# Convolution taps that read a projection's products in PSUM, with weight splits of 1024 columns, in the token mixer of a two-block transformer kernel

## The chip, the cores and the metric

The kernel runs on one core of one Trainium2 chip. The metric is the device time of one execution in microseconds, and the number given for a kernel is the median of its runs. The engines are named as the profile names them: PE is TensorE (PEld its weight loads), DVE is VectorE, ACT is ScalarE, POOL is GpSimd and SP is SyncE, which only starts transfers here.

## What is computed

256 tokens of 1024 features go through two blocks. The first is a layer norm, a token mixer, a norm, a mixture of 32 experts (two per token) and a norm; the second has two layers of attention with feed-forward parts. The mixer has two branches, a spatial gating unit and a gated delta rule over eight heads. The part that the change touches makes the delta rule's q, k and v:

```python
proj = h @ w_in + b_in
...
qkv = jax.nn.silu(_causal_dwconv(dn_qkv, dn_conv_w)).astype(jnp.float32)
q, k, vv = jnp.split(qkv, [DN_KEY, 2 * DN_KEY], axis=-1)
...
q = q * lax.rsqrt(jnp.sum(q * q, -1, keepdims=True) + L2_EPS)
k = k * lax.rsqrt(jnp.sum(k * k, -1, keepdims=True) + L2_EPS)
```

The convolution is causal, four taps deep, one filter per feature: token t of a feature is the sum of tokens t-3 to t, each with its own weight, and tokens before the first are zero. The bias `b_in` is added before the convolution, so the zeros ahead of the first token have no bias in them. For all tokens but the first three the bias adds the same constant, bias times the sum of the four weights; for the first three it adds less.

## The kernel before

**Three stretches.** By the timeline the mixer and the norm in front of it take the first 380 us or so, the mixture of experts runs to about 828 us, and the second block takes the rest. The change lies in the mixer.

**A dense** (`dense`, lines 277 to 325) multiplies the tokens by 512 columns of a weight matrix, over eight chunks of 128 features. Its float32 weights arrive in raw tiles of 1 MB (2048 columns, a ring of five buffers) that SP asks for. Each raw tile is split, 512 columns at a time, into a high part `wh` (line 248, a rounding copy by ACT) and a low part `wl`, the rest (line 249, a subtraction by DVE, or by POOL where `lo_eng` says so). The pool `sp` has five buffers of each. A product is then three matmuls: high by high (line 309, or 319), low tokens by high weights (311, or 321), high tokens by low weights (312, or 320). In the form with features on the partitions ("fm") a dense has 96 matmuls of 256 columns, in the form with tokens on them ("tm") 48 of 512. The result stands in one of two PSUM buffers (`pd`, 128 x 1024) until the function `consume` has read it. Smaller products use four PSUM buffers `pt`, which the profile calls ps.

**The convolution stage** (lines 444 to 484) runs six denses, s = 0 to 5: two each for q, k and v. The function `conv` consumes each: ACT copies each quarter of the PSUM buffer with bias into `pre` in SBUF (line 468) and also makes the fourth tap of it, scaled and with bias, in `cv` (line 469); DVE adds the other three taps of each quarter, reading `pre` (line 471, twelve instructions a dense); ACT applies silu (line 473); POOL squares the result for the norms of q and k (line 476). POOL also clears the three zeros ahead of each `pre` (line 463) and makes one low part in four, one in two in dense 0. PE sums the squares (`sums`, lines 453 to 456), four matmuls behind the next dense. `cv` stands in slot 8 and `sq` in slot 9, one buffer each.

**Behind it** come two denses for z and four for the gates, which a list `Z` holds until they are put between the steps of the delta rule: the score matrices (lines 555 to 569), and the inverse of a triangular matrix, first 32 x 32 blocks on DVE, then two levels of products (lines 607 to 635). A step of a level is a product (line 615), a mask by DVE (618), one or two products with the masked one (624, 629), and subtractions by DVE (631, 633). Lines 645 and after use the inverse.

**Order.** Each engine runs its instructions in the order of its own program. A scheduler sets that order when the kernel is built, from priorities and from buffers; the source doesn't write it out. A change of one instruction's engine or size can thus move others on all engines. The mixture of experts fetches its weights into the mixer's slots and the ring as these come free, which is before the mixer's end.

## Time and profile before

| | |
|---|---|
| median of three runs | 1444.41 us (1443.34 to 1444.89) |
| span of the profiled execution | 1444.6 us |
| mixer | 0 to about 380 us |
| mixture of experts | about 380 to 828 us |
| second block | 828 us to the end |

The profile gives for each instruction its start, its duration and, where its engine was idle before it, how long and what ended the wait. The duration of a pipelined instruction overlaps the next one's start, so the time that a run of them takes is the distance of their starts. [...] The windows sum busy time per engine in a stretch. A wait names the last semaphore that came.

### The profile page before, as it was taken

How to read it: one execution, taken by the hardware profiler on the slowest of the kernel's cores; microseconds unless marked ns; L12 is line 12 of the kernel's file. 1: busy time of each engine (PE TensorE's matmuls, PEld its weight loads, DVE VectorE, ACT ScalarE, POOL GpSimd, SP SyncE). 2: the span in 40 equal slices, each digit the busy share in tenths (PEclk: the TensorE clock that was granted, in tenths of full speed). 3: DMA queues.
4: the chain of work that ended last, by engine and by line, in shares of the span. 5: the costliest groups of instructions: out<-in, count | busy, mean ns of one | idle time of the engine just before them, and what ended most of it. 6: DMA issues, size and time to landing. Idle time of an engine off the chain costs nothing.

```text
span 1444.6 us, 24989 instructions
## 1 busy us (share of the span) xinstructions
PE 1254.9 (87%) x10074; PEld 1001.7 (69%) x10077; DVE 760.0 (53%) x1516; ACT 574.6 (40%) x1165; POOL 137.6 (10%) x118
## 2 busy tenths in 40 slices
PE   5999999699588778767778669999999999999997
PEld 4987988698444434324334248779998887899985
DVE  6897955976611111201101078756666568666664
ACT  3775635444201101101101035655555548655553
POOL 2431000400200000000000021410000013100000
PEclk9999999899799979989889879999999999999998
DMA  7453542388599999999999935245554552455550
GB/s 289 146 175 106 205 158 88 121 338 316 210 419 419 419 411 419 419 420 419 419 419 419 420 132 201 88 146 179 184 192 164 197 209 88 146 176 185 194 176 29
DMA packets 58967, 356.18 MB, mean 247 GB/s; under 512 B 13312, under 2 KB 13824, under 8 KB 17632
## 3 DMA queue, kind: packets, MB, share of 16 engines
q1 hardware_dynamic: 57072, 347.09, 63.3%
q0 software_dynamic: 1488, 6.92, 1.3%
q8 instruction: 81, 1.33, 0.4%
q10 hardware_dynamic: 288, 0.52, 0.1%
q14 instruction: 38, 0.31, 0.1%
HBM read 352.68 MB, written 1.84 MB: 245 GB/s over the span
## 4 chain that ended last, share of the span: by engine, by line
PE 34%; DMA 20%; DVE 4%; ACT 2%; issue 1%; POOL 1%; DVEq 0%; SPq 0%; ACTq 0%
DMA xw<-in_w_dram 16%; PE pd L311 7%; PE pd L312 7%; PE pd L309 7%; DMA raw<-in_w_dram 4%; PE pd L320 4%; PE pd L321 4%; PE pd L319 4%; ACT s L1198 1%; PE ps L1221 1%; PE ps L1181 1%; DVE wl L249 1%; PE ps L1215 0%; DVE s L1186 0%; POOL s L1205 0%
## 5 line engine op out<-in xcount | busy, mean ns | idle before, releaser
L248 ACT ACTIVATE wh<-raw 128x512 fp32r<-128x512 f32 (+1 forms) x532 | 331.0, 631 | 332.6 <-PE pd L311 160.0
L249 DVE TENSOR_TENSOR wl<-raw,wh 128x512 fp32r<-128x512 f32 x497 | 357.8, 727 | 190.2 <-ACT wh L248 187.9
L312 PE MATMUL pd<-xh,wl 128*128 128x256 f32 x1232 | 350.2, 284 | 8.6 <-DVE wl L249 7.0
L309 PE MATMUL pd<-xh,wh 128*128 128x256 f32 x1232 | 348.3, 283 | 0.0
L311 PE MATMUL pd<-xl,wh 128*128 128x256 f32 x1232 | 348.2, 283 | 0.0
L312 PEld LDWEIGHTS pd<-xh,wl 128*128 128x128 f32 x1232 | 232.3, 189 | 12.5 <-DVE wl L249 8.5
L309 PEld LDWEIGHTS pd<-xh,wh 128*128 128x128 f32 x1232 | 233.7, 190 | 1.9 <-issue 1.6
L311 PEld LDWEIGHTS pd<-xl,wh 128*128 128x128 f32 x1232 | 233.1, 189 | 1.9 <-issue 1.4
L1004 DVE COPY hs<-ps 128x256 f32<-128x256 f32 x32 | 13.6, 424 | 265.5 <-PE ps L1000 265.5
L1000 PE MATMUL ps<-xw,xe 128*32 128x256 f32 x1568 | 111.8, 392 | 23.8 <-DMA xw<-in_w_dram 22.0
L1000 PEld LDWEIGHTS ps<-xw,xe 128*32 128x32 f32 x1568 | 53.0, 111 | 65.1 <-DMA xw<-in_w_dram 31.7
L1010 ACT ACTIVATE hx<-ps 128x128 f32<-128x128 f32 x32 | 8.9, 277 | 217.0 <-PE ps L1007 217.0
L249 POOL TENSOR_TENSOR wl<-raw,wh 128x512 fp32r<-128x512 f32 (+1 forms) x35 | 52.8, 1511 | 391.8 <-ACT wh L248 374.8
L1021 PE MATMUL pd<-ys,cst 128*32 128x256 f32 x256 | 71.2, 428 | 15.8 <-ACT ys L1019 15.2
L1015 PE MATMUL ps<-xw,hx 128*32 128x256 f32 x752 | 58.6, 457 | 20.7 <-DVE hx L1011 14.5
L1021 PEld LDWEIGHTS pd<-ys,cst 128*32 128x32 f32 x256 | 28.3, 121 | 59.6 <-ACT ys L1019 34.5
L320 PE MATMUL pd<-wl,hh 128*128 128x512 f32 x176 | 68.6, 390 | 0.0
L321 PE MATMUL pd<-wh,hl 128*128 128x512 f32 x176 | 68.6, 390 | 0.0
L319 PE MATMUL pd<-wh,hh 128*128 128x512 f32 x176 | 68.5, 389 | 0.0
L321 PE MATMUL pd<-wh,xl 128*128 128x512 f32 (+2 forms) x144 | 55.4, 385 | 2.6 <-DVE xl L275 2.6
L320 PE MATMUL pd<-wl,xh 128*128 128x512 f32 (+2 forms) x144 | 56.3, 391 | 1.5 <-DVE wl L249 1.5
L1015 PEld LDWEIGHTS ps<-xw,hx 128*32 128x32 f32 x752 | 24.5, 126 | 47.4 <-DVE hx L1011 20.1
(445 smaller groups left out, 1852.0 us busy)
## 6 DMA issues: line engine op xcount, KB each, us to landing
xw<-in_w_dram SPq DMA_DIRECT2D x145, 1024.0 KB, 19.9
raw<-in_w_dram SPq DMA_DIRECT2D x47, 1024.0 KB, 19.9
raw<-in_gu_dram SPq DMA_DIRECT2D x44, 1024.0 KB, 5.0
raw<-in_w_in_dram SPq DMA_DIRECT2D x32, 1024.0 KB, 4.9
raw<-in_dn_dram SPq DMA_DIRECT2D x20, 1024.0 KB, 4.8
raw<-in_e_b_dram SPq DMA_DIRECT2D x6, 1024.0 KB, 5.4
bc<-in_big_dram POOLq DMA_DIRECT2D x8, 512.0 KB, 5.9
raw<-in_w_pb_dram SPq DMA_DIRECT2D x4, 1024.0 KB, 5.0
```

The source lines that it names most:

```text
L248: self.nc.scalar.activation(hi, src, AF.Copy)
L249: (eng or self.nc.vector).tensor_tensor(lo, src, hi.bitcast(F32), op=OP.subtract)
L309: nc.tensor.matmul(o, a, xh[:, kc, :], start=(kc == 0 and oc % 2 == 0), stop=False, skip_group_check=True)
L311: nc.tensor.matmul(o, a, xl[:, kc, :], start=False, stop=False, skip_group_check=True)
L312: nc.tensor.matmul(o, b, xh[:, kc, :], start=False, stop=(kc == nk - 1), skip_group_check=True)
L319: nc.tensor.matmul(o, xh[:, kc, ts], a, start=(kc == 0), stop=False, skip_group_check=True)
L320: nc.tensor.matmul(o, xh[:, kc, ts], b, start=False, stop=False, skip_group_check=True)
L321: nc.tensor.matmul(o, xl[:, kc, ts], a, start=False, stop=(kc == nk - 1), skip_group_check=True)
L1000: T.matmul(ph[32 * c:32 * c + 32, :256], xe[:, kc, ei * 32:ei * 32 + 32], wt[kc // 2][:, kc % 2, c * 256:(c + 1) * 256], start=(kc == 0), ...
L1015: T.matmul(py[32 * c:32 * c + 32, :256], hx[:, fc % 2, (fc // 2) * 32:(fc // 2) * 32 + 32], wt[4 + fc // 2][:, fc % 2, c * 256:(c + 1) * 2 ...
L1021: T.matmul(pz[32 * ei:32 * ei + 32, c * 256:(c + 1) * 256], ident[:, 32 * c:32 * c + 32], ys, start=True, stop=True, skip_group_check=True)
L1181: T.matmul(ps[:, t * 128:t * 128 + 128 * (t + 1)], q[:, t * 128:t * 128 + 128], k[:, :128 * (t + 1)], start=(t == 0 and j == 0), stop=(j = ...
```

## The change

- The copy `pre` and the pool `conv` are gone. DVE's twelve taps read the products in PSUM, without bias, at 253 to 255 columns each (line 480 of the new kernel); the tokens that a shift would leave out are simply not written.
- The bias comes in with the fourth tap: the constant `bw` is now the bias times the sum of all four weights, and a small table `cut` holds what the first three tokens got too much. One subtraction by DVE per dense corrects them (line 475), before the taps.
- The square moves from POOL to ACT (line 485), and all low parts of the stage are made by DVE. POOL has nothing left in the stage.
- In the mixer the splits are 1024 columns wide, with three buffers instead of five; in the second block they stay 512 wide with five.

Behind the convolution the lines of the new kernel are those of before plus 8. The core of the diff:

```diff
-        step = max(1, 512 // ncol)
+        step = max(1, self.wide // ncol)
...
-                wh = self.sp.tile([128, 512], F32R, name="wh", tag="wh")
-                wl = self.sp.tile([128, 512], F32R, name="wl", tag="wl")
+                wh = self.sp.tile([128, self.wide], F32R, name="wh", tag="wh")
+                wl = self.sp.tile([128, self.wide], F32R, name="wl", tag="wl")
...
-            self.sp = pool("sp", 5)
+            self.sp, self.wide = pool("sp", 5), 512
...
-        self.sp = sp_es.enter_context(tc.tile_pool(name="sp", bufs=5))
+        self.sp, self.wide = sp_es.enter_context(tc.tile_pool(name="sp", bufs=3)), 1024
...
-        with tc.tile_pool(name="conv", bufs=2) as cv:
+        if True:
             wc = self.par("conv").rearrange("p (c k) -> p c k", k=4)
             bw = small.tile([128, 24], F32, name="bw")
+            cut = small.tile([128, 24, 3], F32, name="cut")
+            V.tensor_mul(cut[:, :, 2], self.par("b_qkv"), wc[:, :, 0])
+            V.tensor_mul(cut[:, :, 1], self.par("b_qkv"), wc[:, :, 1])
+            V.tensor_add(cut[:, :, 1], cut[:, :, 1], cut[:, :, 2])
+            V.tensor_mul(cut[:, :, 0], self.par("b_qkv"), wc[:, :, 2])
+            V.tensor_add(cut[:, :, 0], cut[:, :, 0], cut[:, :, 1])
             V.tensor_mul(bw, self.par("b_qkv"), wc[:, :, 3])
+            V.tensor_add(bw, bw, cut[:, :, 0])
...
                 def conv(ps, s=s, dst=dst):
-                    pre = cv.tile([128, 4, 260], F32, name="pre", tag="pre")
-                    P.memset(pre[:, :, 0:3], 0.0)
                     c_ = slot("cv", 8, 8, 256)[:, :4]
                     for oc in range(4):
                         c = s * 4 + oc
-                        p_ = ps[:, oc * 256:(oc + 1) * 256]
-                        S.activation(pre[:, oc, 3:259], p_, AF.Identity, bias=self.par("b_qkv", c))
-                        S.activation(c_[:, oc], p_, AF.Identity, bias=bw[:, c:c + 1], scale=wc[:, c, 3:4])
+                        S.activation(c_[:, oc], ps[:, oc * 256:(oc + 1) * 256], AF.Identity, bias=bw[:, c:c + 1],
+                                     scale=wc[:, c, 3:4])
+
+                    V.tensor_tensor(c_[:, :, 0:3], c_[:, :, 0:3], cut[:, s * 4:s * 4 + 4], op=OP.subtract)
+                    for oc in range(4):
+                        c = s * 4 + oc
                         for kk in range(3):
-                            V.scalar_tensor_tensor(c_[:, oc], pre[:, oc, kk:kk + 256], wc[:, c, kk:kk + 1],
-                                                   c_[:, oc], op0=OP.mult, op1=OP.add)
+                            sh = 3 - kk
+                            V.scalar_tensor_tensor(c_[:, oc, sh:], ps[:, oc * 256:(oc + 1) * 256 - sh], wc[:, c, kk:kk + 1],
+                                                   c_[:, oc, sh:], op0=OP.mult, op1=OP.add)
                     S.activation(dst, c_, AF.Silu)
                     if s < 4:
                         sq = slot("sq", 9, 8, 256)[:, :4]
-                        P.tensor_tensor(sq, dst, dst, op=OP.mult)
+                        S.activation(sq, dst, AF.Square)
                         sqs.append((s, sq))
-                self.dense(A["w_in"][4 + s], 512, 8, xh, xl, "fm", conv,
-                           lo_eng=lambda i, s=s: P if i % 4 == 3 or (s == 0 and i % 2) else None)
+                self.dense(A["w_in"][4 + s], 512, 8, xh, xl, "fm", conv)
```

The scheduler's order changes with it. In the rows below, a name with its number is one buffer, and the name left of the arrow is written. On ACT, from the silu of conv 0 on, before:

```order
L473 ACTIVATE q_183<-cv_386 128x1024
L248 ACTIVATE wh_592<-raw_574 128x512
L248 ACTIVATE wh_608<-raw_574 128x512
L248 ACTIVATE wh_624<-raw_574 128x512
L248 ACTIVATE wh_642<-raw_640 128x512
L468 ACTIVATE pre_543<-pd_410,prm_86 128x256
L469 ACTIVATE cv_545<-pd_410,bw_248,prm_86 128x256
```

The silu of a conv and the first reads of the next dense's PSUM buffer have four high parts between them. On ACT, from the last high part ahead of the silu of conv 1 on, after:

```order
L248 ACTIVATE wh_738<-raw_736 128x1024
L482 ACTIVATE q_183<-cv_510 128x1024
L485 ACTIVATE sq_529<-q_183 128x1024
L472 ACTIVATE cv_652<-pd_535,bw_245,prm_86 128x256 x4
L248 ACTIVATE wh_766<-raw_736 128x1024
L248 ACTIVATE wh_822<-raw_820 128x1024
```

Silu and square of a conv now stand directly ahead of the four reads of the next dense's PSUM buffer. On DVE, around the end of conv 3's taps (buffer cv_871), before:

```order
L249 TENSOR_TENSOR wl_969<-raw_966,wh_968 128x512
L471 SCALAR_TENSOR_TENSOR cv_871<-pre_869,prm_86,cv_871 128x256 x11
L249 TENSOR_TENSOR wl_985<-raw_966,wh_984 128x512
L471 SCALAR_TENSOR_TENSOR cv_871<-pre_869,prm_86,cv_871 128x256
L249 TENSOR_TENSOR wl_1001<-raw_966,wh_1000 128x512
L249 TENSOR_TENSOR wl_1064<-raw_1061,wh_1063 128x512
```

A conv's taps come nearly in a block, and low parts follow them. On DVE, from the last taps of conv 1 (buffer cv_510) to those of conv 2 (cv_652), after:

```order
L249 TENSOR_TENSOR wl_739<-raw_736,wh_738 128x1024
L480 SCALAR_TENSOR_TENSOR cv_510<-pd_393,prm_86,cv_510 128x254
L480 SCALAR_TENSOR_TENSOR cv_510<-pd_393,prm_86,cv_510 128x255
L475 TENSOR_TENSOR cv_652<-cv_652,cut_246 128x4x3
L480 SCALAR_TENSOR_TENSOR cv_652<-pd_535,prm_86,cv_652 128x253
L480 SCALAR_TENSOR_TENSOR cv_652<-pd_535,prm_86,cv_652 128x254
L480 SCALAR_TENSOR_TENSOR cv_652<-pd_535,prm_86,cv_652 128x255
```

The last tap of a conv is now followed at once by the next conv's correction, with no low part between them. On PE, in the first of the two levels of the triangular inverse, before (pd_1823 is a gate's dense):

```order
L309 MATMUL pd_1823<-xh_137,wh_1940 128x256
L624 MATMUL ps_2259<-tf_2257,XT_1991 128x128 x4
L629 MATMUL ps_2264<-XT_1991,tf_2257 128x128 x4
L615 MATMUL ps_2271<-X_1990,la1_1989 128x128 x4
L311 MATMUL pd_1823<-xl_138,wh_1940 128x256
L312 MATMUL pd_1823<-xh_137,wl_1941 128x256
L309 MATMUL pd_1823<-xh_137,wh_1940 128x256
```

Behind a step's product (L615) eight matmuls of the dense stand before the next step reads the mask's result. On PE, in the same level, after (pd_2433 is a gate's dense):

```order
L321 MATMUL pd_2433<-wh_2486,xl_138 128x512
L623 MATMUL ps_2033<-X_1771,la0_1769 128x128
L632 MATMUL ps_2040<-tf_2038,XT_1772 128x128 x4
L637 MATMUL ps_2045<-XT_1772,tf_2038 128x128 x4
L623 MATMUL ps_2052<-X_1771,la1_1770 128x128 x4
L632 MATMUL ps_2059<-tf_2057,XT_1772 128x128 x4
L637 MATMUL ps_2064<-XT_1772,tf_2057 128x128 x4
```

The dense's matmuls are all ahead of these steps, which follow each other directly. From the branch in the mixture of experts on, the orders of all engines are those of before.

## Rows read from the trace of the kernel before

**Rows 1.** Section 1 of the page: busy us, share of the span, instructions.

```profile
PE 1254.9 (87%) x10074; PEld 1001.7 (69%) x10077; DVE 760.0 (53%) x1516; ACT 574.6 (40%) x1165; POOL 137.6 (10%) x118
```

**Rows 2.** Windows: bounds, length, each engine's busy us (instructions), PE clock, DMA, GB/s.

```profile
40.00:60.00 20.00, 19.80 (x168) 18.86 (x168) 19.07 (x33) 15.68 (x29) 9.65 (x7) 1.00 0.44 153
...
300.00:320.00 20.00, 20.00 (x173) 20.00 (x172) 13.38 (x23) 8.88 (x14) 0.00 (x0) 1.00 0.87 331
```

**Rows 3.** Timeline of ACT: start, us, what it is, idle before and its releaser.

```profile
38.26 0.46 ACT L468 ACTIVATE pre<-pd,prm 128x256 f32<-128x256 f32 x1
...
96.12 1.07 ACT L473 ACTIVATE v<-cv 128x1024 f32<-128x1024 f32 x1 [2.53 <-DVE cv L471]
...
100.52 0.46 ACT L468 ACTIVATE pre<-pd,prm 128x256 f32<-128x256 f32 x1
100.88 0.56 ACT L469 ACTIVATE cv<-pd,bw,prm 128x256 f32<-128x256 f32 x1
101.33 0.47 ACT L468 ACTIVATE pre<-pd,prm 128x256 f32<-128x256 f32 x1
```

**Rows 4.** Groups by line, 20:110 us: count, busy us, mean ns, idle before.

```profile
L249 DVE TENSOR_TENSOR wl<-raw,wh 128x512 fp32r<-128x512 f32 x40 | 37.0, 951 | 6.1 <-ACT wh L248 6.1
...
L473 ACT ACT_TABLE_LOAD x2 | 2.6, 1283 | 0.0
...
L272 DVE TENSOR_SCALAR tf<-ps,prm 128x256 f32<-128x256 f32 x5 | 2.5, 534 | 0.0
```

**Rows 5.** Groups by line and shape, DVE, 285 to 300 us.

```profile
L249 DVE TENSOR_TENSOR wl<-raw,wh 128x512 fp32r<-128x512 f32 x7 | 4.7, 684 | 1.1 <-ACT wh L248 1.1
L765 DVE SCALAR_TENSOR_TENSOR tf<-ps,prm,bc 128x256 f32<-128x256 f32 x8 | 3.6, 479 | 0.1
```

**Rows 6.** Timeline of DVE, three places.

```profile
47.47 4.26 DVE L249 TENSOR_TENSOR wl<-raw,wh 128x512 fp32r<-128x512 f32 x3 [0.45 <-ACT wh L248]
51.65 4.57 DVE L471 SCALAR_TENSOR_TENSOR cv<-pre,prm,cv 128x256 f32<-128x256 f32 x11
...
174.34 1.13 DVE L600 COPY XTs<-Xs 64x1024 f32<-64x1024 f32 x1
```

**Rows 7.** Timeline of POOL in the convolution.

```profile
48.84 1.73 POOL L249 TENSOR_TENSOR wl<-raw,wh 128x512 fp32r<-128x512 f32 x1
```

**Rows 8.** Instructions of L471: ns min/median/max, first and last start.

```profile
L471 DVE SCALAR_TENSOR_TENSOR cv<-pre,prm,cv x72: 470/478/1524, 39.2 to 106.1; 128x256 f32<-128x256 f32 x72
```

**Rows 9.** Waits of PE, 20 to 110 us: total us, times, longest.

```profile
PE pd L312 <- DVE wl L249: 2.2, 3, 1.2
```

**Rows 10.** Timeline of PE, first matmuls behind two stops.

```profile
263.07 0.58 PE L312 MATMUL pd<-xh,wl 128*128 128x256 f32 x1 [3.52 <-DVE wl L249]
...
875.34 0.31 PE L1343 MATMUL ps<-cst,ca 128*128 128x128 f32 x1 [3.08 <-issue]
```

**Rows 11.** Windows of 2 us behind the two stops.

```profile
262.00:264.00 2.00, 0.93 (x4) 0.94 (x5) 2.00 (x9) 0.00 (x0) 0.97 (x2) 0.50 0.14 53
...
876.00:878.00 2.00, 2.00 (x13) 2.00 (x12) 1.28 (x3) 0.70 (x2) 0.00 (x0) 0.56 1.00 311
878.00:880.00 2.00, 2.00 (x12) 2.00 (x11) 1.64 (x5) 0.95 (x3) 0.00 (x0) 0.58 0.83 311
```

**Rows 12.** Waits of PE, 14 to 380 us.

```profile
PE pd L320 <- DVE wl L249: 1.5, 1, 1.5
PE ps L629 <- DVE XT L633: 1.4, 1, 1.4
...
PE ps L645 <- DVE XT L633: 0.9, 1, 0.9
...
PE ps L624 <- DVE tf L618: 0.4, 1, 0.4
```

**Rows 13.** Timeline of DVE in the levels.

```profile
217.73 0.69 DVE L618 TENSOR_TENSOR tf<-ps,mixc 128x512 f32<-128x512 f32 x1 [0.21 <-PE ps L615]
```

**Rows 14.** A window at the mixer's end; section 2's transfer rate in 40 slices.

```profile
GB/s 289 146 175 106 205 158 88 121 338 316 210 419 419 419 411 419 419 420 419 419 419 419 420 132 201 88 146 179 184 192 164 197 209 88 146 176 185 194 176 29
...
386.00:388.00 2.00, 2.00 (x12) 2.00 (x11) 0.82 (x2) 0.71 (x2) 0.00 (x0) 0.50 0.00 0
```

## Prediction

> **What bounds the kernel now.** I read the busy shares first [rows 1]: TensorE 87%, no other engine near it. An average over three stretches with different limits says little, so next came the windows of the first stretch, the mixer, in which every edited line lies. Two of 20 us show its limits [rows 2]: at 300 us TensorE is busy 20.00 of 20 with 173 matmuls, the pace of a TensorE-bound stretch; at 40 us, in the convolution, it starts 168 while VectorE is busy 19.07. So the convolution is nearly TensorE-bound with VectorE close behind, and the question is which of the two the change makes late.
>
> The pace gives the price of one dense: 20/173 = 0.116 us a matmul, 96 matmuls, 11.1 us, and with the sums of squares between (4 matmuls side by side, about 0.4) 11.5. What it takes now: the first copy out of PSUM of dense 0 starts at 38.26 and that of dense 5 at 100.52 [rows 3], so five denses take 62.3 us, 12.45 each. At most 62.3 - 57.5 = 4.8 us can be won in the stage if TensorE never waits.
>
> Then I looked at how VectorE spends its time. A 512-wide low part has a mean of 951 ns in this stretch [rows 4], but 684 ns in a stretch where GpSimd is idle [rows 5]; three in a row took 4.26 us from 47.47 [rows 6], across the start of a low part of GpSimd's own at 48.84 [rows 7]. So GpSimd's work there costs VectorE time, and the change takes it away. That speaks for a gain. What speaks against is the order on ScalarE and VectorE.
>
> **The change part by part.** PSUM's hold. Before, a dense's PSUM buffer is free after eight short ScalarE copies. After, the taps read it, so it is free after VectorE's last tap, and with two buffers dense s+2 cannot start until conv s has had its last tap. The cycle from one conv's first VectorE instruction (L475) to the next thus becomes a limit of TensorE. Its parts: after the last tap VectorE has, in most cycles, nothing but L475 ahead, which waits for all four L472; on ScalarE these stand behind silu and the square, each 1024 wide at 1.07 us (0.96 from start to start), and the four take 0.45 each by the starts 100.88 and 101.33 [rows 3]. 0.96 + 0.96 + 1.8 with handoffs of 0.15 is 3.9 us. L475 itself is tiny, 0.2. Twelve taps: eleven take 4.57 now [rows 6], 0.41 each from start to start, 4.9 in all. A tap out of PSUM is not in the trace; the same operation with a PSUM source in the gating stage takes 479 ns [rows 5] against a median of 478 for today's taps [rows 8], so I add nothing; the dearest row with a PSUM source of this width, 534 ns [rows 4], would add 12 x 0.055 = 0.7 a cycle. Four 1024-wide low parts: the nearest row is a copy of 1024 columns, 1.13 [rows 6], and two narrow ones end to end would be 2 x 0.684 = 1.37; I take 1.14, near the row of the same width, 4.6 in all. VectorE waits some 0.5 for high parts, since three buffers of 1024 let ScalarE run less far ahead. Sum: 3.9 + 0.2 + 4.9 + 4.6 + 0.5 = 14.1 us, against TensorE's 11.5. With the best of each (a low part in the silu's shadow in every cycle, no wait for high parts) it is about 12.5; with PSUM's dearest price and 1.37 a low part, 15.7.
>
> From dense 0's end (D0) the first L475 starts at D0 + 2.9 (one wide high part stands ahead of the first L472). Conv 3's last tap is three cycles and the rest of one later: 2.9 + 3 x 14.1 + 10.2 = D0 + 55.4. Dense 5 may start then and ends 11.8 later, at D0 + 67.2; before it was D0 + 62.3. **+4.9 us**, between -1.5 (a cycle of 12.5: 2.9 + 37.5 + 8.6 + 11.8 = 60.8) and +11.3 (15.7: 2.9 + 47.1 + 11.8 + 11.8 = 73.6).
>
> The clock. TensorE will then stand still in about two places (ahead of denses 3 and 5) for some 3 us each, where it now waits 2.2 us in three waits over the whole stage [rows 9]. The trace has such stops, of 3.52 us (to 263.07) and 3.08 us (to 875.34) [rows 10]. Behind the second the granted clock fell to about half: 0.56 and 0.58 in the four us from 876, which lack 0.88 + 0.84 = 1.7 us of full clock [rows 11]. Dense 5's falls wholly on the path; part of dense 3's is swallowed by the next wait. Between 0 and 3.4; I take **+2.2**. [...]
>
> Square on ScalarE, six tiny VectorE operations, no GpSimd. The square is in the cycle. The tiny operations (products of 24 columns) stand ahead of the conv: +0.3 at most. GpSimd's leaving is in the 1.14 already.
>
> Table loads. In the new order of ScalarE the norms' logarithm and the last silus alternate: three loads more than before until z's last silu, 1.28 each [rows 4], 3.8 us. They come when TensorE has z's first dense (11 us) before it: 0 if that covers them, 3.8 if not; I take 0.
>
> Behind the conv. z's first dense loses today's wait for a low part, 1.5 at L320 [rows 12], and gets one for conv 4's last tap, D0 + 69.5 against TensorE there at 67.2 plus the sums and the score's transposes: about 0.8 new. -0.7.
>
> The level chain. L615, L618, L629 and L633 (after: 623, 626, 637 and 641) multiply by levels: each product waits for VectorE's mask or subtraction. Before, matmuls of a z or gate dense stand between its steps in TensorE's order; after, that dense is all ahead of it, and the steps stand bare. Each of seven bare steps waits for 0.69 of VectorE and two handoffs of 0.1 to 0.2 [rows 13], 0.9: 6.4 us. Of today's waits there, 1.4 (L629), 0.9 (L645) and 0.4 (L624), 2.7, go in return [rows 12]. **+3.7**, between 0 and +5.
>
> What follows is TensorE's own pace (20.00 of 20 at 300 us) and gives nothing back. Nor does the MoE: at 386 us the transfers stand at 0 GB/s, as all buffers are full, and then run at 411 to 420 in twelve slices of 36 us [rows 14]; they start when the mixer's results are there, so a late mixer makes a late MoE, one to one. From the MoE on all engines' orders are those of before.
>
> Sum: 4.9 + 2.2 + 0.3 - 0.7 + 3.7 = 10.4. The profiled execution's span is 1444.6, 0.2 above the median of 1444.41, so 1444.6 + 10.4 = **1455.0 us**.
>
> **The rivals.** A, faster: the hold never binds. If ScalarE's chain fits behind other VectorE work, so that the cycle is 11.7 or less, TensorE runs at its pace: 5 x 11.7 = 58.5 against 62.3, -3.8, and with the level chain paid for by the denses ahead of it 1440.8. For it: VectorE's own work in a cycle is only 9.7 us, and the relief of 0.27 us on each low part is real. Against: the order of VectorE puts L475 right behind the last taps in most cycles. It decides at 11.7 us.
>
> B, a wash: cycle near 12.5, where it is today; no stops, clock full: 1444.6 + 0.3 - 0.7 and 0 to 2 of the level chain, about 1445.
>
> C, worse: both clock falls at full price (+1.2), table loads bare (+3.8): 1460.
>
> D, taps dearer out of PSUM at 0.534: 0.7 a cycle, four cycles, +2.8: 1457.8. [...]
>
> Does the change do what it says? The order shows that the copies and all GpSimd work leave the stage, so there is no rival there.
>
> **How the numbers follow.** Forecast 0.56 (1449 to 1459), A 0.10, B 0.14, C 0.10, D 0.10. Below 1445 lie A and a third of B, 0.14; above 1461 some 0.05: the range is 1445 to 1461. A measurement of this kernel can tell 0.2%, 2.9 us, from no change. Faster by more is A, 0.10; within is most of B, 0.12; slower is the rest, 0.78.
>
> **What would show it.** In the profile after: L309 waiting for VectorE's taps (L480) ahead of denses 3 and 5 for about 3 us; L475 waiting for L472 nearly 4 us in two or more cycles; first L472 of conv 0 to that of conv 5 about 67 us or more; the granted clock under 1.00 in the 60 to 100 us windows; L480 at 478 ns; wide low parts at 1.14; L632 and L637 waiting 0.9 each, seven times; the transfers starting again some 10 us later. Wrong it is if L309 doesn't wait, if the square or silu runs while VectorE has low parts to do, or if the time lost here is won back before the MoE's transfers start.

## The result and the profile after

The changed kernel takes 1464.71 us, median of four runs (1461.13 to 1467.41), against 1443.88 for the kernel before: a ratio of 1.0133, 95% interval 1.0118 to 1.0148. It is slower, as forecast, but by 20.8 us and not by 10.6, and the time lies outside the stated range. The profiled execution, 1461.13 us with a span of 1459.3, is the shortest of the four; against the span of before (1444.6) it lost 14.7. A run's time is 1.8 us more than its span, so the profiled execution of before took about 1446.4 us, 2.5 above its median of 1443.88, and that of after lies 3.6 below its own: the 6.1 us between the two differences come from which executions were profiled. The account below explains the 14.7.

Section 1 of the page of after, busy us and share of the span, against [rows 1]:

```profile
PE 1260.3 (86%) x10074; PEld 1004.3 (69%) x10077; DVE 746.0 (51%) x1454; ACT 561.0 (38%) x1060; POOL 104.5 (7%) x94
```

Every engine but TensorE has less to do, and the kernel is slower: the work that was saved is not what TensorE waits for. The waits of PE from 14 to 397 us (us in total, times, longest), which answer to [rows 9] and [rows 12], show where:

```profile
PE pd L312 <- DVE wl L249: 10.1, 2, 9.8
PE pd L309 <- DVE cv L480: 7.7, 3, 3.8
PE ps L401 <- DVE tf L272: 3.3, 1, 3.3
PE pd L319 <- DVE cv L480: 2.4, 2, 1.2
PE ps L632 <- DVE tf L626: 2.4, 3, 0.8
PE ps L637 <- DVE tf L626: 2.3, 3, 0.8
```

L309 waiting for a tap (L480) is the hold of PSUM: before dense 3 and dense 5, 3.8 and 3.3 us. L632 and L637 are the bare level chain. The L312 with 9.8 us stands where before had 3.5 and 7.8, behind the norm of the delta rule's output. The L401 with 3.3 us is one that the prediction does not have; it was under a microsecond before.

ACT and DVE between conv 1 and conv 2 (start, us, what it is, idle before and its releaser) show the cycle's bad half:

```profile
70.37 1.06 ACT L482 ACTIVATE q<-cv 128x1024 f32<-128x1024 f32 x1 [2.75 <-DVE cv L480]
71.46 1.06 ACT L485 ACTIVATE sq<-q 128x1024 f32<-128x1024 f32 x1
72.42 1.92 ACT L472 ACTIVATE cv<-pd,bw,prm 128x256 f32<-128x256 f32 x4
```

```profile
66.01 2.29 DVE L480 SCALAR_TENSOR_TENSOR cv<-pd,prm,cv 128x255 f32<-128x255 f32 x5
68.21 1.21 DVE L249 TENSOR_TENSOR wl<-raw,wh 128x1024 fp32r<-128x1024 f32 x1
69.34 0.99 DVE L480 SCALAR_TENSOR_TENSOR cv<-pd,prm,cv 128x254 f32<-128x254 f32 x2
74.37 0.17 DVE L475 TENSOR_TENSOR cv<-cv,cut 128x12 f32<-128x12 f32 x1 [4.04 <-ACT cv L472]
```

From the last tap to L475 VectorE stands still for 4.04 us while ScalarE does silu, square and four L472, one behind the other. This L475 and the one before it wait so in full (4.04 and 4.06 us); ahead of the last two another instruction splits the idle time (2.14 and 1.54 around a low part; 4.37 ahead of L516). The L475 of convs 0 to 4 start at 45.19, 59.91, 74.37, 88.74 and 104.05: a cycle of 14.4 to 15.3 us.

TensorE meanwhile stood still. Windows of 2 us around dense 3's start at 70.48 (bounds, length, busy us and instructions of five engines, then PE's granted clock as a share of full speed, DMA share and GB/s):

```profile
68.00:70.00 2.00, 0.00 (x0) 0.00 (x0) 1.96 (x4) 0.00 (x0) 0.00 (x0) 1.00 0.91 381
70.00:72.00 2.00, 1.51 (x7) 1.55 (x8) 0.34 (x1) 1.60 (x2) 0.00 (x0) 0.50 0.16 66
72.00:74.00 2.00, 2.00 (x15) 1.07 (x15) 0.00 (x0) 2.00 (x5) 0.00 (x0) 0.65 0.00 0
74.00:76.00 2.00, 2.00 (x19) 2.00 (x18) 1.55 (x5) 0.82 (x2) 0.00 (x0) 1.00 0.00 0
```

After the stop the clock is 0.50 and comes back within four microseconds; 2 x 0.50 + 2 x 0.35 = 1.7 us of full clock are gone.

**An account that closes.** For each profile I summed PE's waits from 16 us to the matmul with which the experts' selection starts (L924, or L932), without the wait of the first transposes, and the full-clock time that a low clock took from a busy PE (busy us x (1 - granted clock), in windows of 1 us). What is left of the start of the selection is nearly the same in all versions, 355 to 360 us: the first 16 us, the wait directly ahead of the selection (12.8 to 13.5 us, not in the column of waits) and TensorE's own work. The mixer's length is that plus TensorE's other waits plus its lost clock.

| version | median us | ratio to before, 95% interval | dense 1, dense 5 start | selection starts | waits | lost clock | rest |
|---|---|---|---|---|---|---|---|
| before | 1443.88 to 1445.64 by group | 1 | 37.6, 87.3 | 380.6 | 22.6 | 2.4 | 355.6 |
| after | 1464.71 | 1.0133 (1.0118 to 1.0148) | 42.1, 99.5 | 397.0 | 33.2 | 6.9 | 356.9 |
| after, again (e5) | 1462.45 | 1.0112 (1.0090 to 1.0134) | 43.8, 102.2 | 400.9 | 33.3 | 11.3 | 356.3 |
| e1 narrow splits | 1458.82 | 1.0093 (1.0068 to 1.0119) | 40.0, 97.5 | 395.0 | 30.1 | 4.9 | 360.0 |
| e2 wide splits alone | 1451.30 | 1.0042 (1.0023 to 1.0062) | 42.7, 93.6 | 386.3 | 25.8 | 5.0 | 355.5 |
| e3 SBUF copy back | 1449.60 | 1.0039 (1.0022 to 1.0055) | 41.9, 94.1 | 386.5 | 24.6 | 5.2 | 356.7 |
| e4 two cv | 1461.03 | 1.0111 (1.0089 to 1.0133) | 43.1, 99.7 | 396.1 | 32.1 | 8.5 | 355.5 |
| e6 narrow and copy | 1433.30 | 0.9915 (0.9897 to 0.9932) | 38.5, 87.9 | 367.4 | 10.0 | 0.5 | 356.9 |
| e7 GpSimd in dense 0 only | 1441.77 | 0.9976 (0.9965 to 0.9987) | 37.6, 85.0 | 378.4 | 20.5 | 2.7 | 355.2 |
| e8 = e6 + GpSimd in dense 0 | 1431.81 | 0.9911 (0.9892 to 0.9930) | 40.4, 89.8 | 368.6 | 9.4 | 0.2 | 359.0 |
| e9 PSUM taps alone | 1457.06 | 1.0069 (1.0052 to 1.0087) | 39.6, 91.2 | 396.6 | 29.6 | 7.6 | 359.4 |
| e10 before, h on VectorE | 1436.79 | 0.9926 (0.9904 to 0.9947) | 37.1, 86.7 | 373.1 | 13.4 | 3.1 | 356.6 |
| e11 after, h on VectorE | 1456.17 | 1.0068 (1.0044 to 1.0093) | 42.7, 102.2 | 394.1 | 26.9 | 11.6 | 355.6 |
| e12 = e8, h on VectorE | 1429.48 | 0.9882 (0.9865 to 0.9898) | 39.7, 89.1 | 367.4 | 8.4 | 1.4 | 357.6 |

Between before and after the waits grew by 10.6 us and the lost clock by 4.5, 15.1 of the 16.4 by which the selection starts later. From there to the end 1.7 us come back.

### The profile page after: what moved, and what is told of

Same layout as the page of the kernel before. It is cut to its first block, busy times and chain, and to the rows that moved or that the text cites. A ratio compares the mean times of both kernels' runs of the same rounds, so it can differ in the third digit from the quotient of the medians.

```text
span 1459.3 us, 24651 instructions
## 1 busy us (share of the span) xinstructions
PE 1260.3 (86%) x10074; PEld 1004.3 (69%) x10077; DVE 746.0 (51%) x1454; ACT 561.0 (38%) x1060; POOL 104.5 (7%) x94
## 4 chain that ended last, share of the span: by engine, by line
PE 35%; DMA 20%; DVE 4%; ACT 2%; issue 1%; POOL 0%; SPq 0%; DVEq 0%; ACTq 0%
DMA xw<-in_w_dram 13%; PE pd L311 7%; PE pd L309 7%; PE pd L312 7%; DMA raw<-in_w_dram 6%; PE pd L321 4%; PE pd L320 4%; PE pd L319 4%; PE ps L1229 1%; ACT s L1206 1%; DMA raw<-in_e_b_dram 1%; PE ps L1189 1%; DVE wl L249 1%; PE ps L1223 1%; DVE s L1194 0%
## 5 line engine op out<-in xcount | busy, mean ns | idle before, releaser
L248 ACT ACTIVATE wh<-raw 128x512 fp32r<-128x512 f32 (+2 forms) x444 | 315.7, 715 | 344.9 <-PE pd L311 181.2
L249 DVE TENSOR_TENSOR wl<-raw,wh 128x512 fp32r<-128x512 f32 (+2 forms) x423 | 343.9, 817 | 195.9 <-ACT wh L248 193.5
L312 PE MATMUL pd<-xh,wl 128*128 128x256 f32 x1232 | 349.4, 284 | 11.7 <-DVE wl L249 10.1
L309 PE MATMUL pd<-xh,wh 128*128 128x256 f32 x1232 | 350.0, 284 | 7.7 <-DVE cv L480 7.7
L312 PEld LDWEIGHTS pd<-xh,wl 128*128 128x128 f32 x1232 | 234.1, 190 | 14.0 <-DVE wl L249 10.5
L309 PEld LDWEIGHTS pd<-xh,wh 128*128 128x128 f32 x1232 | 234.0, 190 | 12.6 <-issue 12.3
L319 PE MATMUL pd<-wh,hh 128*128 128x512 f32 x176 | 68.5, 389 | 0.0
L319 PE MATMUL pd<-wh,xh 128*128 128x512 f32 (+2 forms) x144 | 56.9, 395 | 2.4 <-DVE cv L480 2.4
```

The lines of the kernel that those rows point to most:

```text
L248: self.nc.scalar.activation(hi, src, AF.Copy)
L249: (eng or self.nc.vector).tensor_tensor(lo, src, hi.bitcast(F32), op=OP.subtract)
L309: nc.tensor.matmul(o, a, xh[:, kc, :], start=(kc == 0 and oc % 2 == 0), stop=False, skip_group_check=True)
L312: nc.tensor.matmul(o, b, xh[:, kc, :], start=False, stop=(kc == nk - 1), skip_group_check=True)
L319: nc.tensor.matmul(o, xh[:, kc, ts], a, start=(kc == 0), stop=False, skip_group_check=True)
```

## The experiments

**e1, narrow splits.** After, with one line of the mixer undone:

```diff
-self.sp, self.wide = sp_es.enter_context(tc.tile_pool(name="sp", bufs=3)), 1024
+self.sp, self.wide = sp_es.enter_context(tc.tile_pool(name="sp", bufs=5)), 512
```

> The changed kernel with the mixer's splits 512 wide and five buffers again; all else of the change stays. Theory 1 (the wide splits stand ahead of the first conversions of the tokens and delay dense 0 by about 4 us): the first L472 comes near 39 us instead of 43.2, the time falls by 4 to 5 us against the changed kernel's 1464.7, to about 1460; L309 still waits for L480 ahead of denses 3 and 5, 3 us each. Rival (the start is late because GpSimd no longer makes low parts there, or because of the six small operations): the first L472 stays at 42 to 43 us and the time within 1.5 us of 1464.

Measured: 1458.82 us. The first L472 comes at 40.7 instead of 43.2 and L401 waits 0.9 us instead of 3.3, so the wide splits, with their three buffers, make the long wait at the start. Dense 1 starts at 40.0, sooner than after's 42.1 but still 2.4 us later than in before; e8 shows most of that. L309 still waits, 5.6 us in four waits, and the time is 5.9 us under after's. The other two thirds of the loss have another cause.

**e2, wide splits alone.** Before, with the diff's lines on `self.wide` and three buffers, nothing else (the other uses of 512 in the split follow).

```diff
-step = max(1, 512 // ncol)
+step = max(1, self.wide // ncol)
...
-self.sp = sp_es.enter_context(tc.tile_pool(name="sp", bufs=5))
+self.sp, self.wide = sp_es.enter_context(tc.tile_pool(name="sp", bufs=3)), 1024
```

> The kernel before with one part of the change alone: splits 1024 wide with three buffers in the mixer. Taps still read the SBUF copy, GpSimd still squares and makes one low part in four. Theory 1: the first L468 comes at 41 to 43 us instead of 38.3 and the time is 1447 to 1450; no L309 waits for a tap. Rival (width is no cost): 38 to 39 us and 1443 to 1445.

Measured: 1451.30 us, 6 to 7 above before (1444.35 in its group) and 1.3 above the expected range. Dense 1 starts at 42.7 instead of 37.6. Its first matmuls behind the conversion of the tokens (timeline of PE):

```profile
20.71 0.91 PE L401 MATMUL ps<-xh,wab 128*32 128x256 f32 x8 [2.73 <-DVE tf L272]
22.46 1.07 PE L401 MATMUL ps<-xl,wab 128*32 128x256 f32 x4 [0.83 <-DVE xl L275]
```

In all six profiles with wide splits (after, e5, e2, e3, e4, e11) the first L401 waits 2.7 to 3.4 us; in the eight with narrow ones 0.7 to 1.3. In after the reason is on VectorE:

```profile
16.32 1.23 DVE L249 TENSOR_TENSOR wl<-raw,wh 128x1024 fp32r<-128x1024 f32 x1 [0.72 <-ACT wh L248]
17.46 0.99 DVE L272 TENSOR_SCALAR tf<-ps,prm 128x256 f32<-128x256 f32 x2
20.27 1.23 DVE L249 TENSOR_TENSOR wl<-raw,wh 128x1024 fp32r<-128x1024 f32 x1 [1.82 <-ACT wh L248]
21.41 0.99 DVE L272 TENSOR_SCALAR tf<-ps,prm 128x256 f32<-128x256 f32 x2
22.32 1.28 DVE L275 TENSOR_TENSOR xl<-tf,xh 128x512 fp32r<-128x512 f32 x2
```

Two wide low parts stand ahead of the first low token part (L275), and the second waits 1.82 us for its high part, which ScalarE makes between conversions of its own. TensorE's next matmuls (L401) wait for L272, 3.3 us, and the clock falls behind this stop too (0.50 from 23 to 25 us). In e2 only one wide low part stands there; its L272 waits 1.38 us for ScalarE's L271, which stands behind a wide high part. So it is the wide splits ahead of the token conversions, on one engine or the other.

**e3, the SBUF copy back.** After, with ScalarE's copy and taps that read it:

```diff
+                    pre = slot("pre", 5, 8, 256)[:, :4]
+                    for oc in range(4):
+                        S.activation(pre[:, oc], ps[:, oc * 256:(oc + 1) * 256], AF.Copy)
...
-V.scalar_tensor_tensor(c_[:, oc, sh:], ps[:, oc * 256:(oc + 1) * 256 - sh], wc[:, c, kk:kk + 1],
+V.scalar_tensor_tensor(c_[:, oc, sh:], pre[:, oc, :256 - sh], wc[:, c, kk:kk + 1],
```

> The changed kernel with ScalarE's copy of the products back (four more instructions a dense, without bias, in slot 5), from which the taps read; splits stay wide, GpSimd stays out, the square stays on ScalarE. Theory (PSUM is held until the last tap): no L309 waits for VectorE any more, denses 0 to 5 take about 60 to 62 us again, the clock stays at 1.00 there, and the time falls by 7 to 9 us to about 1456. Rival (the cycle of VectorE and ScalarE itself sets the end, whoever holds PSUM): the waits move to L312 or L320 and the time stays within 2 us of 1464.

Measured: 1449.60 us, 15 below after, twice what was expected; no L309 waits for a tap. From dense 1's start to dense 5's it is 52.2 us, against 57.3 in after and 49.7 before. The clock did not stay full: at 61 and 62 us TensorE had two short waits (0.80 and 0.75 us), and 1.7 us of clock went behind them. The experiment undoes the hold. The selection starts 10.5 us sooner than in after; 5.1 us of that are there by dense 5's start, and most of the rest comes right behind it, where after has the clock of dense 5's stop and the waits of L319 and L560. So with wide splits and all low parts on VectorE the hold is the largest part of the loss.

The experiment also compares taps by source, first after, then e3:

```profile
62.03 0.86 DVE L480 SCALAR_TENSOR_TENSOR cv<-pd,prm,cv 128x255 f32<-128x255 f32 x2
69.34 0.99 DVE L480 SCALAR_TENSOR_TENSOR cv<-pd,prm,cv 128x254 f32<-128x254 f32 x2
```

```profile
45.17 4.82 DVE L483 SCALAR_TENSOR_TENSOR cv<-pre,prm,cv 128x253 f32<-128x253 f32 x12
```

Each quarter has a tap of 253, one of 254 and one of 255 columns. At 62.03 a quarter's last tap (255) is followed by another quarter's first (253), 0.39 us later; at 69.34 a tap of 254 by the one of 255 of the same quarter, 0.51 us later. The taps of e3 alternate between two quarters, and all follow at 0.39 to 0.41.

**e4, two buffers for cv.** After, with convs taking turns between two places for cv.

```diff
-c_ = slot("cv", 8, 8, 256)[:, :4]
+c_ = slot("cv", (8, 5)[s % 2], 8, 256)[:, :4]
```

> The changed kernel with two buffers for cv (slot 8 and slot 5 in turn), so that the four L472 of a dense need not stand behind silu and square of the one before. Theory (after the last tap VectorE stands idle while ScalarE does silu, square and four L472, 3.9 us of the 14.5 us cycle): L475's wait falls from 4 us to under 2, the cycle to about 12.5, L309's waits of 3.8 and 3.3 to at most 1.5 in all but dense 3, and the time falls by 4 to 6 us to about 1459. Rival (the scheduler puts the L472 behind silu all the same, or the taps alone set the cycle): within 1.5 us of 1464.

Measured: 1461.03 us, 3.7 below after by medians, with overlapping intervals; the profile's span is that of after's (1459.4 against 1459.3). The cycle did what the theory says in one place only. Conv 2's L472 now come ahead of conv 1's silu (ACT, then DVE):

```profile
68.33 1.92 ACT L472 ACTIVATE cv<-pd,bw,prm 128x256 f32<-128x256 f32 x4
71.27 1.06 ACT L482 ACTIVATE q<-cv 128x1024 f32<-128x1024 f32 x1 [1.02 <-DVE cv L480]
```

```profile
70.28 0.17 DVE L475 TENSOR_TENSOR cv<-cv,cut 128x12 f32<-128x12 f32 x1 [0.20 <-ACT cv L472]
70.37 6.05 DVE L480 SCALAR_TENSOR_TENSOR cv<-pd,prm,cv 128x253 f32<-128x253 f32 x13
78.97 1.23 DVE L249 TENSOR_TENSOR wl<-raw,wh 128x1024 fp32r<-128x1024 f32 x1 [2.55 <-ACT wh L248]
```

L475 waits 0.20 instead of 4.04, and that cycle is 9.7 us. But dense 3 had already waited 3.9 us at 71.4, its clock was low until 79 (0.50 from 73 on), and so the next cycle takes 19.7 (L475 at 70.28 and 90.01). For convs 1 and 4 the scheduler left three of the four L472 behind silu and square. The chain is real where it stands; a second buffer does not take it away as long as the order is not changed with it.

**e5, after once more.** No edit.

> The changed kernel itself, unchanged, beside the others of this group. Its runs so far lay between 1461.1 and 1467.4, the profiled one being the shortest. Theory (the order of instructions makes the loss, so it is the same in every run): L401 waits 3.3 us at the start, L309 3.8 and 3.3 us ahead of denses 3 and 5, and the transfers of the experts start some 16 us later than before, give or take 1. Rival (a part of the loss lies elsewhere and comes and goes): another stretch, the experts' or the second block's, differs between the two profiles of this kernel by over 2 us.

Measured: 1462.45 us (1458.67 to 1464.07), a span of 1462.3 in the profile, 3.0 above that of after's first. The rival's sign, another stretch, is not there: the selection starts 3.9 us later than in the first profile, so all of it is in the mixer. The waits are the same (33.3 against 33.2); what differs is how long the clock stayed low behind the same stops:

```profile
72.00:74.00 2.00, 2.00 (x9) 1.96 (x9) 0.00 (x0) 1.97 (x3) 0.00 (x0) 0.50 0.00 0
74.00:76.00 2.00, 2.00 (x13) 1.00 (x12) 0.12 (x2) 1.85 (x5) 0.00 (x0) 0.50 0.00 0
76.00:78.00 2.00, 2.00 (x13) 2.00 (x13) 1.80 (x5) 0.00 (x0) 0.00 (x0) 0.63 0.00 0
```

From dense 3's start at 72.00 the clock was low until 78, where the first profile has it back at 74. Behind each of the three new stops (L401, denses 3 and 5) the granted clock lacks 1.7 us in the first profile and 3.4 in the second, 5.1 and 10.2 in all; 4.8 and 9.1 of it fell on a busy TensorE, as the table counts it. That is a spread of over 4 us between executions of one program, about half of what the runs of after show (1458.67 to 1467.41).

**e6, narrow splits and the copy.** After, with e1's and e3's edits. What stays of the change is that GpSimd is out of the stage, the square on ScalarE and the corrected bias.

> The changed kernel with both costly parts undone: splits 512 wide with five buffers, and taps that read ScalarE's SBUF copy. What stays of the change: no GpSimd in the stage, the square on ScalarE, the corrected bias. Theory (the loss is the hold of PSUM plus the wide splits, and GpSimd's leaving costs 2 to 2.5 us in dense 0 and gains up to 4 behind it): dense 1 starts at 40 us, dense 5 at 86 to 88, and the time is 1442 to 1447. Rival (VectorE without GpSimd's help is late): L312 waits for low parts in each dense, over 4 us in all, and the time is over 1449.

Measured: 1433.30 us, 0.85% below before and 9 to 14 us below what the theory gave. Denses 1 and 5 start at 38.5 and 87.9, as before, so the stage gains nothing. The gain comes further on, most of it some 150 us later, and e10 asks for that.

**e7, GpSimd in dense 0 only.** Before, with GpSimd's low parts in dense 0 alone.

```diff
-           lo_eng=lambda i, s=s: P if i % 4 == 3 or (s == 0 and i % 2) else None)
+           lo_eng=lambda i, s=s: P if s == 0 and i % 2 else None)
```

> The kernel before with one part of the change, cut to where it should help: GpSimd makes low parts in dense 0 only (every other one, as before) and none in denses 1 to 5; it still squares. Theory (GpSimd's low parts slow VectorE's by 0.27 us each, but its help is needed in dense 0): dense 1 starts at 37.6 us as before, L312's 2.2 us of waits go, dense 5 starts 2 to 4 us sooner than 87.3, and the time is 1441 to 1443 if the rest of the mixer keeps it. Rival (those waits are nothing to the end): 1443.5 to 1445.

Measured: 1441.77 us, ratio 0.9976 (0.9965 to 0.9987). Dense 1 starts at 37.6, dense 5 at 85.0 (87.3 before), and no L312 waits in the stage. GpSimd's low parts did cost VectorE and, through it, TensorE 2.3 us; 2.2 of that reach the selection.

**e8, e6 with GpSimd's low parts in dense 0.**

```diff
-self.dense(A["w_in"][4 + s], 512, 8, xh, xl, "fm", conv)
+self.dense(A["w_in"][4 + s], 512, 8, xh, xl, "fm", conv,
+           lo_eng=lambda i, s=s: P if s == 0 and i % 2 else None)
```

> As the version with narrow splits and the SBUF copy, but GpSimd makes every other low part of dense 0 again. Theory (dense 0 is late by 2.4 us where VectorE makes all its low parts): dense 1 starts at 37.6 us instead of 40, and the time is 2 us below that version's. Rival (the three or four matmuls at the start wait for something else): dense 1 starts at 39.5 to 40.5 and the time is the same within 1 us.

Measured: 1431.81 us, against e6's 1433.30; but dense 1 starts at 40.4, not at 37.6, and e6 without GpSimd at 38.5. So VectorE alone is not what makes dense 0 late in the narrow versions, and my reading of that part was wrong. The traces show what does. TensorE's first matmuls behind the conversion, in e8 with the window around them, then in e6:

```profile
20.83 1.08 PE L401 MATMUL ps<-xl,wab 128*32 128x256 f32 x4
21.84 0.58 PE L311 MATMUL pd<-xl,wh 128*128 128x256 f32 x1
20.00:22.00 2.00, 2.00 (x13) 0.55 (x13) 2.00 (x5) 2.00 (x6) 0.41 (x2) 1.00 1.01 422
```

```profile
20.49 0.63 PE L401 MATMUL ps<-xl,wab 128*32 128x256 f32 x4 [0.18 <-DVE xl L275]
21.05 0.38 PE L311 MATMUL pd<-xl,wh 128*128 128x256 f32 x1
```

In e8 they take 1.08 and 0.58 us instead of 0.63 and 0.38. That is what they take in after, where the clock column reads 0.50 (1.08 and 0.58 at 23.05 and 24.06), but here it reads 1.00. e1, e9 and e12 have the same stretch, from the first L401 to about 23 or 24 us. From start to start, without waits, dense 0's matmuls and L401 take 18.5 to 18.8 us together in these four, 17.1 in e6 and 16.0 to 16.3 in before, e7 and e10. So the start lost 1.4 to 1.7 us to TensorE's pace, which the table has under rest. What brings this stretch about in four of the eight narrow versions is open; their waits ahead of it are 0.7 to 0.9 us, as in before.

**e9, PSUM taps alone.** The diff's conv alone. Against after, what goes back to before is the split, the square and GpSimd's low parts:

```diff
-self.sp, self.wide = sp_es.enter_context(tc.tile_pool(name="sp", bufs=3)), 1024
+self.sp, self.wide = sp_es.enter_context(tc.tile_pool(name="sp", bufs=5)), 512
...
-S.activation(sq, dst, AF.Square)
+P.tensor_tensor(sq, dst, dst, op=OP.mult)
...
-self.dense(A["w_in"][4 + s], 512, 8, xh, xl, "fm", conv)
+self.dense(A["w_in"][4 + s], 512, 8, xh, xl, "fm", conv,
+           lo_eng=lambda i, s=s: P if i % 4 == 3 or (s == 0 and i % 2) else None)
```

> The kernel before with one part of the change alone: the taps read the products in PSUM with the corrected bias. Splits are 512 wide with five buffers, GpSimd makes its low parts and the squares as before. Theory (holding PSUM until the last tap is the larger part of the loss, whatever the splits): L309 waits for L480 ahead of denses 3 and 5, the five denses from 1 on take 6 to 9 us more than the 62 us of before, the clock falls there, and the time is 1452 to 1462. Rival (the hold costs only together with wide splits or without GpSimd): L309's waits stay under 1 us and the time within 2 us of before.

Measured: 1457.06 us, in the expected range, but not for the expected reason. From dense 1's start to dense 5's it is 51.6 us against 49.7, with one L309 wait of 1.9 us. By the prediction's own sum, without the square (0.96) and one low part in four (1.14), the cycle is 14.1 - 2.1 = 12.0, little above TensorE's 11.5; measured it is 12.7 to 14.4, and TensorE also waits 2.9 us there for GpSimd's squares (L462). So in the stage the hold costs much only together with the work that the change moved to ScalarE and VectorE. Even so this part of the change alone loses 11.5 us, and most of that comes behind the stage: short waits at 112 to 115 us and 5.1 us of clock after them, a bare level chain, and the stop behind the output's norm:

```profile
PE ps L718 <- ACT o L711: 8.5, 1, 8.5
PE ps L633 <- DVE tf L627: 2.7, 3, 1.1
PE ps L638 <- DVE tf L627: 2.3, 3, 0.8
```

```profile
114.00:116.00 2.00, 1.21 (x2) 0.65 (x4) 1.40 (x4) 2.00 (x5) 0.00 (x0) 0.80 0.00 0
116.00:118.00 2.00, 1.83 (x8) 1.70 (x8) 2.00 (x6) 1.45 (x4) 0.00 (x0) 0.50 0.00 0
```

**e10, before with h on VectorE.** In e6 TensorE waits 1.2 us for the output's norm (L720 there), where before waits 7.8 behind a 3.5, and all of GpSimd's products o x zs come ahead of its products of h. In before they alternate (timeline of POOL, then one of VectorE's small operations of a norm, two columns wide):

```profile
254.36 1.74 POOL L697 TENSOR_TENSOR o<-o,zs 128x512 f32<-128x512 f32 x1
256.06 2.92 POOL L751 TENSOR_TENSOR h<-h,bc 128x1024 f32<-128x1024 f32 x1
259.90 2.48 POOL L697 TENSOR_TENSOR o<-o,zs 128x512 f32<-128x512 f32 x2
263.41 4.70 POOL L753 TENSOR_TENSOR h<-h,bc 128x1024 f32<-128x1024 f32 x2 [1.03 <-DMA bc<-in_big_dram]
```

```profile
259.24 0.16 DVE L220 TENSOR_TENSOR nr_z<-nr_z,nr_t 128x2 f32<-128x2 f32 x1
259.44 2.98 DVE L222 SCALAR_TENSOR_TENSOR nr_w<-nr_z,nr_y 128x2 f32<-128x2 f32 x1
```

An operation of two columns, 0.16 us otherwise, takes 2.98 while GpSimd works from 259.90 on, and ends at 262.41, where GpSimd ends at 262.38. That norm has five such slow operations of two columns in before, 1.26 to 2.98 us, and five in after; each of the ten ends 0.02 to 0.03 us behind the end of an operation of GpSimd. The edit, in L751 and L753:

```diff
-P.tensor_tensor(h[:, t], h[:, t], g_bc, op=OP.mult)
+V.tensor_tensor(h[:, t], h[:, t], g_bc, op=OP.mult)
...
-P.tensor_tensor(h[:, t], h[:, t], b_bc, op=OP.add)
+V.tensor_tensor(h[:, t], h[:, t], b_bc, op=OP.add)
```

> The kernel before with the four products and sums of h (L751, L753, 1024 columns each) on VectorE instead of GpSimd; nothing of the change. It asks why the version with narrow splits and SBUF copy is 12 us below the kernel before, when undoing the change's losses only gives before's time. Theory (before, GpSimd's h operations stand between the products o x zs, slow VectorE's small operations of the norm from 0.2 to over 2 us, and so hold L709; in that version all four o x zs come first): o's norm ends near 255 instead of 272, L709's wait of 7.8 us and the 6.8 us of lost clock go, and the time falls by 8 to 13 us. Rival (the version gains by its faster convolution and its order of z and gates): within 3 us of before.

Measured: 1436.79 us, ratio 0.9926. The wait for the norm falls from 7.8 to 2.5 us, the norm's scaling (L702) starts at 264.0 instead of 272.0, as the theory had it; the time falls by 8.7 us, within its 8 to 13. The clock is no part of that: it lacks 1.7 us there instead of 6.8, but only 2.3 of the 6.8 fell on a busy TensorE, and the table has 3.1 us of lost clock against 2.4. VectorE does the four operations at 1.21 us each; GpSimd took 2.35 to 2.92.

**e11, after with h on VectorE.** The same edit.

> The changed kernel with the same four operations on VectorE. Its L312 waits 9.8 us at 287 us behind the same operations. Theory: that stop goes, and the time falls by 6 to 12 us from the changed kernel's 1462 to 1465; the difference to the version of before with the same edit stays 15 to 20 us. Rival: the stop was only waiting for work that is late anyway, and the time falls by less than 3 us.

Measured: 1456.17 us (1450.71 to 1461.73). The 9.8 us stop is gone, 3.2 remain, and the time falls by 6.3 to 8.5 us, by the two medians of after. The distance to e10 is 19.4 us: the change's own loss does not depend on that stop.

**e12, the best version.** e8 with the same edit.

> The version with narrow splits, SBUF copy and GpSimd's low parts in dense 0 only, with the four h operations on VectorE too. There all four products o x zs already stand ahead of the h operations. Theory (nothing is left to gain from GpSimd's h operations where they don't stand between): 1430 to 1433, as that version's 1431.8. Rival (GpSimd slows VectorE there too): 1425 to 1429.

Measured: 1429.48 us, ratio 0.9882 (0.9865 to 0.9898), 2 below e8, with overlapping runs, and 16 below before. It lies between the theory's 1430 to 1433 and the rival's 1425 to 1429 and decides neither.

## Why the prediction was wrong in size and right in kind

- **Hold and cycle: right.** Predicted 14.1 us a cycle, measured 14.4 to 15.3; 3.9 us of idling VectorE, measured 4.0 in two of the five cycles and in two pieces in two more; waits of some 3 us ahead of denses 3 and 5, measured 3.8 and 3.3. From dense 1's start to dense 5's last matmul the stage takes 70.8 us against 62.2, 8.6 more, where the terms of hold and clock summed to 7.1.
- **A tap's price: the row was right, the pace was not.** The duration is 476 ns against 478, as the row of the gating stage had it. But in after a tap behind one of the same quarter starts 0.51 us after it (27 pairs), and only behind another quarter's tap 0.40 (18 pairs). Both paces are there with an SBUF source too: 0.39 in e3, whose taps alternate, and 0.51 to 0.52 between the first two taps of each conv in before. So the pace goes with the order of the taps, and the runs don't show that the source sets it. By an estimate from these pairs, 27 x 0.11 / 6, it costs 0.5 us a cycle that the sum left out. Rival D's price of 0.7 was near in size, but not for D's reason.
- **The failed step is the start.** "The tiny operations (products of 24 columns) stand ahead of the conv: +0.3 at most" looked for the change's cost at the start in the operations added there and not in those made wider, which got no term at all. Dense 1 starts 4.6 us late in the profiled execution, 6.2 in the second. e1 and e2 show that the wide splits make it: without them L401's stop of 3.3 us is back at 0.9, and alone they bring dense 1 to 42.7. That they do so by standing ahead of L272 and L275 is read from the orders of VectorE and ScalarE. It could have been read before: in the old order one low part, 512 wide, stands ahead of the first L275, in the new one two of 1024.
- **The clock was mis-sized.** The term was 2.2 for two stops, between 0 and 3.4. There are three new stops, the third being the start's (four narrow versions have a low pace there too, behind a stop of 0.7 to 0.9 us, see e8), and behind each the clock lacks 1.7 us or 3.4, depending on the execution: 5.1 to 10.2, of which 4.8 to 9.1 on a busy TensorE. The trace of before had one row of it (1.7 behind 3.08 us), and beside it 6.8 between 261 and 276 us (2.3 on a busy TensorE), which should have warned that a stop has no single price.
- **Together.** The span grew by 14.7 us where the sum had 10.4. The start alone is 4.3 above its term (0.3); the other misses (+1.5 in the stage, +2.4 behind it, -0.8 in the levels, some -3 from there to the end) nearly cancel, which is luck. The remaining 5.4 us to the median of 1464.71 come from which executions were profiled; e5, with 4.4 us more of lost clock at the same waits, shows the clock as what varies.
- **Behind the conv: -0.7 was +1.7** (L319 1.2 twice and L560 0.8, against 1.5). **Levels: +3.7 was +2.9** (2.4 + 2.3 + 0.9 against 1.4 + 0.9 + 0.4): six bare steps and not seven, at 0.78 a step.
- **"What follows gives nothing back" held nearly**: the selection starts 16.4 us late, the end comes 14.7 late.
- **Two signs came out otherwise.** From the first L472 of conv 0 to that of conv 5 it is 76.4 us, not about 67: three table loads (1.28 us each) stand ahead of conv 5's while TensorE works on z's first dense. Their term was 0; up to 2.0 us reached TensorE, as L560 waits 0.8 and z's second dense (the L319 at 133.52) waits 1.2 for conv 5's last tap. And the experts' selection starts 16 us later, not some 10.
- **Rivals.** A did not happen: no cycle came under 14.4. Its ground was right, though: freeing VectorE from GpSimd's low parts is worth 2.3 us in the stage (e7). C is the closest to what happened, for its clock and for about half of its table loads. D has the size of the taps' cost and not its cause. The range's upper end, 1461, stood one above C and left out the start.

Not settled: why the scheduler leaves the level chain bare in after, e1, e2, e3, e4, e9 and e11, and not in before, e7 and e10; and why TensorE's pace is low at the start of e1, e8, e9 and e12.

## What to carry to other kernels

Reading a result straight from PSUM saves a copy and keeps the buffer until the slowest reader has finished (here L309 waited 3.8 and 3.3 us for the last tap); before doing it, add up the cycle from one buffer's first read to the next one's, with every instruction of the other engines that stands in it. When operations are made wider, read in each engine's order what they now stand ahead of, above all at the start, where everything waits for one small chain. And where one engine limits a stretch, the stretch is that engine's work plus its waits plus its lost clock (here its work, with the start and the wait ahead of the selection, came to 355 to 360 us in every version): sum these three and the account either closes or shows what was overlooked.

## What the runs showed of the hardware

- Stops of TensorE of some 3 us cost a second time: behind the three new ones of after (3.3, 3.8 and 3.3 us) the granted clock was 0.50, and the same stop of the same program took 1.7 us of full clock in one execution and 3.4 in another.
- The clock column does not show all of it: in e8 TensorE's matmuls took 1.08 and 0.58 us instead of e6's 0.63 and 0.38, as in after at 0.50, while it read 1.00.
- Taps with a PSUM source have the same duration as those with an SBUF source (476 and 478 ns). With either source they follow each other at 0.39 to 0.41 us where the next tap is of another quarter; in after it is 0.51 where it is of the same quarter, which reads what the last tap wrote.
- VectorE's smallest operations took up to 2.98 us instead of 0.16 while GpSimd worked on tensors of 512 and 1024 columns (products and sums), and ended 0.02 to 0.03 us behind the end of GpSimd's operation, ten times of ten. In e10, without GpSimd's h operations, one of the norm's ten operations of two columns took 1.27 us and nine took 0.14 to 0.16, and the wait for the norm fell from 7.8 to 2.5 us.
